# A hybrid decoder layer on one core: an ordered queue of loads and vector-engine weight sums in the down product, two buffers for early results, and stores moved to SyncE

## The chip, the cores and the metric

The kernel runs on one core of a Trainium2 chip. Its engines are TensorE (matrix products, PE in the rows; PEld is its weight load), VectorE (DVE), ScalarE (ACT), GpSimd (POOL) and SyncE (SP), each with its own queue of instructions, which it takes in order. "ACTq" and "SPq" in a row are transfers that ScalarE or SyncE issues. The metric is device time in microseconds (us), the median of several runs. The span of a profiled execution is the time from its first to its last instruction.

## The reference, cut to what matters

One decoder layer on x of shape (1, 1024, 1024): a token mixer, then a SwiGLU feed-forward, each with sandwich RMS norms and gates from a condition vector. The part around the change is the end of the mixer and the feed-forward.

```python
x = x + ga_m * rms_norm(concat(o_a, o_b) @ w_out, g_post_mix)
h = rms_norm(x, g_pre_ffn) * (1.0 + sc_f) + sh_f
gate, up = split(h @ w_gate_up)                 # 1024 x 2816 each
y = (silu(gate) * up) @ w_down                  # 2816 x 1024
x = x + ga_f * rms_norm(y, g_post_ffn)
```

## The kernel before, in words

Every float32 product is made of three products of split operands: `split` (lines 118 and 121) writes a rounded high half (a cast on ScalarE) and the rest as a low half (a subtraction on VectorE or GpSimd), and TensorE multiplies high by high, high by low and low by high. Tiles that hold such pairs are `wgu` (up weights), `hbo`, `hbs` (the activations h and their sums) and `hl` (down part).

The two feed-forward products are computed with seven block products instead of eight, named "1" to "7". Each needs sums of blocks of the weights and of the activations, and sums of the results.

**The end of the mixer.** `out_tile` makes the eight row tiles of x; `mod` and the loop over `k` that follows make h and the block sums T1 to T4 and B22 from it, on ScalarE and VectorE. For the first seven of the 22 column blocks f of the up product (`EARLY`), `early(f)` already multiplies blocks "1" and "2" while these sums are still being made: `product` with B11 into a PSUM bank, a copy of the bank into the left half of a tile `pr`, `product` with B21 onto the same bank, SiLU into the right half, and a store of the tile to `early_d` in DRAM by ScalarE's queue. For f below 3 `pr` is one of two `pair` tiles; for f from 3 to 6 it is the one tile `G_m`.

**The up part.** The loop over `order` takes the remaining block products of all f, 12 matmuls each: "67543" for the early f, "1627543" for the others, 140 in all. `prepare` keeps `LOOK` = 7 weight blocks ready ahead, in eight `wgu` tiles: four in the pool `fab0`, four in `fab1`, whose memory is that of the pool `outp` (`tm`, `G_m`, `xt2`, `HB`). `sources(f)` loads four `rawg` tiles by SyncE's queue and forms four sums on GpSimd (lines 1182 to 1185). VectorE adds up the results (lines 1302 to 1313), GpSimd multiplies (1310, 1315), and `act_sums` forms the activation blocks of the down product (1247, 1253, 1255, 1257), which `store` writes to `asd` in DRAM by ScalarE's queue, 77 blocks of 256 KB. Between them, `ada_acc(5, ...)` forms the gate of the last norm: 16 loads into the `rawg` ring and 16 multiply-adds on VectorE (lines 325, 327).

**The down part.** For w in "162754" and then "3", and for k from 0 to 10, `left` loads an activation block (`adr`, a ring of four) and splits it, `right` brings the weight block and splits it, and `down` issues 12 matmuls (line 1391). The `hl` tiles are a ring of ten, so five k at most are ready ahead. `WE[k]` (`we`) and `WD[k]` (`wo`) hold the weights of k. `right` loads a whole row block of 512 KB (line 1365) for "1", and 256 KB each for "6" and "2" (line 1368). Weight sums run on GpSimd (lines 1374, 1380) and on VectorE (1370, 1372, 1382). `finish` loads x again (`xt`), adds, and stores the output.

The order in each queue is fixed at build time by the framework's list scheduler, which places instructions by its own model of time and by priorities (`low` lowers one), so the code's order isn't the queue's order: a load may be placed well ahead of its use, and in front of loads that are needed sooner.

Of the kernel before, what the change touches and what calls it, by code (L numbers as in the profile page):

```python
# [13 lines left out]
P = 128  # L14
SEQ = 1024
NT = SEQ // P
D = 1024
# [30 lines left out]
def hybrid_layer(ctx, tc, x, c, w_ada, b_ada, g_pre_mix, g_post_mix, g_pre_ffn, g_post_ffn, w_in,  # L48
# [1037 lines left out]
    def pair():  # L1086
        return fsum.tile([P, 2, 512], F32, name="pair", bufs=2)
# [73 lines left out]
    def early(f):  # L1161
        ws = [weights(2 * f + h) for h in range(2)]
        bank = ps_O() if f % 2 else ps_S()

        pr = pair() if f < 3 else op_.tile([P, 2, 512], F32, name="G_m", bufs=1)
        product(bank, ws[0], B11, True, False)
        S.copy(pr[:, 0], bank)  # L1167
        product(bank, ws[1], B21, False, True)
        S.activation(pr[:, 1], bank, AF.Silu)
        nc.scalar.dma_start(early_d[f], pr)  # L1170
# [24 lines left out]
    for t in range(4, NT):  # L1195
        out_tile(t)
        if t > 4:
            early(t - 5)
    T2 = block(otp[1], "o")
    T3, T4 = (block(h2p, "s%d" % j) for j in (3, 4))  # L1200
    T1, B22 = (block(sl, "s%d" % j) for j in (1, 2))
# [35 lines left out]
    even = {}  # L1237

    def store(w, m, a):
        nc.scalar.dma_start(asd[AI[w], m], a)  # L1240

    def act_sums(f, a):

# [41 lines left out]
    for n, (f, w) in enumerate(order):  # L1285
        prepare(n + LOOK)
        early_act(n + 3)
        q = st_.setdefault(f, {})
        key = {"1": "X", "2": "X", "6": "Z", "7": "Z", "4": "Z", "5": "W", "3": "W"}[w]
        if w in "165":  # L1290
            q[key] = {"X": ps_S, "Z": ps_T, "W": ps_O}[key]()
        bank = q[key]
        product(bank, blks.pop(n), HBK[w], w in "165", w in "243")
        if w == "1":
            q["p1"] = half_t("p1", 3)
            S.copy(q["p1"], bank)
        elif w == "2":
            q["act"] = act_t()
            S.activation(q["act"][:, 0:512], bank, AF.Silu)
        elif w == "6":  # L1300
            q["u2"] = half_t("u2", 2)
            V.tensor_tensor(q["u2"], bank, q["p1"], op=OP.add)
        elif w == "7":
            q["u3"] = half_t("u3", 2)
            V.tensor_tensor(q["u3"], bank, q["p1"], op=OP.add)  # L1305
        elif w == "5":
            V.tensor_tensor(q["u3"], bank, q["u3"], op=OP.add)
        elif w == "4":
            V.tensor_tensor(q["p1"], bank, q["p1"], op=OP.add)
            G.tensor_tensor(q["act"][:, 0:512], q["act"][:, 0:512], q["p1"], op=OP.mult)  # L1310
            store("12"[f % 2], f // 2, q["act"][:, 0:512])
        else:
            V.tensor_tensor(q["u2"], bank, q["u2"], op=OP.add)
            S.activation(q["act"][:, 512:1024], q["u2"], AF.Silu)
            G.tensor_tensor(q["act"][:, 512:1024], q["act"][:, 512:1024], q["u3"], op=OP.mult)
            act_sums(f, q["act"])
            st_.pop(f)
        if w == "3" and f == 8:
            acc5 = fca.tile([P, SEQ], F32, name="acc5")
            with low(ADALOW):  # L1320
                ada_acc(5, acc5, fraw, "rawg", 512, 7, nc.sync)
        if w == "3" and f == 11:
            ada_sum(5, acc5)
    for name in ("fca", "fab1", "sl", "fab0", "fsum", "fraw"):
        L.pop(name)
# [20 lines left out]
    nc.gpsimd.dma_start(G_f.rearrange("p a b -> p (a b)"), bcast(gmd, D, D))  # L1346
    X, Z = [ps_S(), ps_S(), ps_T(), ps_T()], [ps_T(), ps_O(), ps_O(), ps_O()]

    def f32(tl, h):
        return tl[:, h, :]  # L1350

    def left(w, k, hl):
        ar = dr.tile([P, 512], F32, name="adr", bufs=4)
        nc.sync.dma_start(ar, asd[AI[w], k])
        split(hl[:, 0], hl[:, 1], ar, S, V)
        return hl

# [2 lines left out]

    def right(w, k):

        e, o = WE[k], WD[k]
        if w == "1":
            nc.sync.dma_start(e.rearrange("p a b -> p (a b)"), w_down[0, 2 * k * P:(2 * k + 1) * P, :])
        elif w in "62":
            h = int(w == "6")
            nc.sync.dma_start(f32(o, h), w_down[0, (2 * k + 1) * P:(2 * k + 2) * P, h * 512:(h + 1) * 512])
        if w == "6":
            V.tensor_tensor(e0(k), f32(o, 1), e0(k), op=OP.subtract)  # L1370
        elif w == "7":
            V.tensor_tensor(f32(e, 1), f32(o, 1), f32(e, 1), op=OP.subtract)
        elif w == "5":
            G.tensor_tensor(e0(k), f32(o, 1), e0(k), op=OP.subtract)
        src = {"1": e0(k), "6": e0(k), "2": f32(o, 0), "7": f32(e, 1), "5": e0(k), "4": f32(o, 0), "3": f32(o, 1)}[w]

        hl = ring() if w != "3" else dw.tile([P, 2, 512], F32R, name="wh", tag=f"we{k}")
        split(hl[:, 0], hl[:, 1], src, S, V)
        if w == "1":
            G.tensor_tensor(e0(k), f32(e, 1), e0(k), op=OP.subtract)  # L1380
        elif w == "2":
            V.tensor_tensor(f32(o, 0), f32(o, 0), e0(k), op=OP.subtract)
        return hl

    def e0(k):
        return f32(WE[k], 0)

    def down(bank, A, B, k, js, first, last):
        for j in js:
# [7 lines left out]
    def finish(t, ca, cb):  # L1397

        tk_ = slice(t * P, (t + 1) * P)
        xt = df.tile([P, D], F32, name="xt3", bufs=3)  # L1400
        nc.sync.dma_start(xt, x2d[tk_, :])
        G.tensor_scalar(ssd[:, t, 2:3], ssd[:, t, 0:1], 1.0 / D, 1e-6, op0=OP.mult, op1=OP.add)
        G.tensor_scalar(ssd[:, t, 3:4], ssd[:, t, 1:2], 1.0 / D, ssd[:, t, 2:3], op0=OP.mult, op1=OP.add)
        r = df.tile([P, 1], F32, name="rfr", bufs=3)
# [99 lines left out]
```

## Time and profile before

| | us |
|---|---|
| median of 3 runs (1574.71 to 1579.72) | 1575.67 |
| the profiled execution, its own time | 1578.7 |
| its span | 1576.7 |
| TensorE busy in it | 1453.8 (92%) |
| VectorE busy | 1203.6 (76%) |
| ScalarE busy | 875.1 (55%) |
| GpSimd busy | 740.3 (47%) |

The profiled execution is one of its own, 3.0 us above the median of the runs; its own time holds 2.0 us around the span. In the timeline, a row is an instruction or a run of like ones, and the bracket says how long its engine sat idle before it and what ended the wait.

### The profile page before, as it was taken

Reading aid. Unit: us, or ns where it says so; the run is one execution under the profiler, and the core shown is the slowest. Engines: PE = TensorE matmul, PEld = TensorE weight load, DVE = VectorE, ACT = ScalarE, POOL = GpSimd, SP = SyncE. Lnnn points to the kernel's source line nnn. Section 1 sums busy time; section 2 is a strip of 40 time slices with the busy share of each in tenths; the row PEclk is TensorE's granted clock in tenths of the full one; section 3 lists DMA queues with packets and bytes.
Section 4 is the critical chain, followed back from the end, with each engine's and each line's share of the span. In section 5 each row is a group of like instructions: output and inputs, shape, how many; then the busy total and the mean of one; then the engine's idle time right before and its main releaser. Section 6 shows DMA issues by size and latency. Waiting matters only on the chain.

```text
span 1576.7 us, 23672 instructions
## 1 busy us (share of the span) xinstructions
PE 1453.8 (92%) x7841; PEld 1232.7 (78%) x7841; DVE 1203.6 (76%) x2639; ACT 875.1 (55%) x1848; POOL 740.3 (47%) x1000
## 2 busy tenths in 40 slices
PE   3899998997889999899999879999999999799998
PEld 3789898996667877788887757887888888588886
DVE  6888988997999998778765585678556544878657
ACT  3447678966777877678774762222323322344543
POOL 2584353646877666355554325654444443423003
PEclk9999999996899999999999888999999999999999
DMA  9471351200000001211126554556333233943335
GB/s 305 147 233 28 60 156 38 85 2 9 9 13 1 1 13 48 67 35 41 41 97 236 192 163 133 161 159 187 102 97 113 92 99 109 372 139 97 98 110 191
DMA packets 141417, 168.65 MB, mean 107 GB/s; under 512 B 17440, under 2 KB 92544, under 8 KB 141168
## 3 DMA queue, kind: packets, MB, share of 16 engines
q1 hardware_dynamic: 119584, 127.60, 26.2%
q10 hardware_dynamic: 21072, 37.43, 6.5%
q0 software_dynamic: 640, 2.13, 0.4%
q8 instruction: 61, 1.00, 0.3%
q14 instruction: 60, 0.49, 0.1%
HBM read 126.71 MB, written 40.41 MB: 106 GB/s over the span
## 4 chain that ended last, share of the span: by engine, by line
PE 57%; DVE 22%; DMA 8%; ACT 6%; issue 4%; POOL 2%; ACTq 0%; SPq 0%; DVEq 0%; POOLq 0%
PE pT L1158 10%; PE pO L1158 7%; PE pS L1158 6%; PE pO L1391 4%; PE pT L1391 4%; PE pS L1391 3%; DVE tk_j L470 3%; DVE p L729 3%; DVE ptl L742 2%; DMA wt<-in_w_ada_dram 2%; PE pT L837 2%; PE pS L721 2%; PE pO L272 2%; PE pO L273 2%; PE pO L274 2%
## 5 line engine op out<-in xcount | busy, mean ns | idle before, releaser
L742 DVE TENSOR_TENSOR ptl<-pT,ptl 128x512 fp32r<-128x512 f32 x228 | 139.6, 625 | 31.7 <-ACT ptl L741 30.7
L1158 PE MATMUL pO<-hbs,wgu 128*128 128x512 f32 x564 | 139.6, 394 | 7.0 <-ACT G_m L1167 7.0
L741 ACT CAST ptl<-pT 128x512 fp32r<-128x512 f32 x228 | 117.6, 541 | 43.2 <-PE pO L842 18.7
L118 ACT CAST wgu<-pair 128x512 fp32r<-128x512 f32 x88 | 53.8, 620 | 153.8 <-PE pT L1158 69.8
L1158 PE MATMUL pT<-hbs,wgu 128*128 128x512 f32 x528 | 128.8, 393 | 4.6 <-DVE u L1305 4.6
L1158 PEld LDWEIGHTS pO<-hbs,wgu 128*128 128x128 f32 x564 | 107.6, 191 | 30.0 <-ACT G_m L1167 7.4
L272 PE MATMUL pO<-wsp,hT 128*128 128x256 f32 (+1 forms) x416 | 120.8, 292 | 10.2 <-ACT kvt L607 4.8
L273 PE MATMUL pO<-wsp,hT 128*128 128x256 f32 (+1 forms) x416 | 119.9, 289 | 5.1 <-DVE wsp L121 5.1
L1158 PEld LDWEIGHTS pT<-hbs,wgu 128*128 128x128 f32 x528 | 99.9, 190 | 26.6 <-DVE u L1305 5.9
L274 PE MATMUL pO<-wsp,hT 128*128 128x256 f32 (+1 forms) x416 | 119.1, 287 | 0.0
L825 POOL TENSOR_SCALAR p<-p,stat,gates 128x640 f32<-128x640 f32 (+7 forms) x128 | 106.3, 845 | 23.2 <-DVE stat L737 16.4
L732 ACT ACTIVATE p<-p,stat 128x640 f32<-128x640 f32 (+7 forms) x128 | 94.0, 736 | 26.7 <-DVE stat L731 17.2
L121 DVE TENSOR_TENSOR wgu<-pair,wgu 128x512 fp32r<-128x512 f32 x88 | 73.4, 839 | 38.1 <-ACT wgu L118 37.9
L118 ACT CAST hl<-adr 128x512 fp32r<-128x512 f32 x77 | 47.5, 623 | 96.4 <-PE pO L1391 40.5
L538 ACT ACTIVATE tk_j<-scores,tk_s 128x384 bf16<-128x384 f32 (+2 forms) x93 | 87.1, 937 | 10.0 <-DVE tk_s L480 3.7
L272 PEld LDWEIGHTS pO<-wsp,hT 128*128 128x128 f32 x416 | 81.1, 196 | 12.6 <-ACT kvt L607 5.6
L118 ACT CAST wgu<-rawg 128x512 fp32r<-128x512 f32 x66 | 40.6, 620 | 85.9 <-PE pT L1158 40.5
L273 PEld LDWEIGHTS pO<-wsp,hT 128*128 128x128 f32 x416 | 81.3, 196 | 6.7 <-DVE wsp L121 5.8
L470 DVE TENSOR_SCALAR_CACHE_REDUCE tk_j<-scores,tk_v 128x512 bf16<-128x512 f32 (+2 forms) x96 | 83.9, 874 | 0.6
L721 PE MATMUL pS<-KK,qst 128*128 128x512 f32 (+3 forms) x192 | 78.0, 411 | 6.8 <-DVE stat L729 6.5
L837 PE MATMUL pT<-ident,p 128*128 128x128 f32 x528 | 82.5, 279 | 1.8 <-POOL p L825 1.2
L1182 POOL TENSOR_TENSOR pair<-rawg 128x512 f32<-128x512 f32 x22 | 29.0, 1319 | 116.2 <-DVE wgu L121 110.2
(498 smaller groups left out, 4615.0 us busy)
## 6 DMA issues: line engine op xcount, KB each, us to landing
rawg<-in_w_gate_up_dram SPq DMA_DIRECT2D x102, 256.0 KB, 3.4
adr<-asd SPq DMA_DIRECT2D x77, 256.0 KB, 2.7
asd<-act ACTq DMA_DIRECT2D x66, 256.0 KB, 3.0
raw<-in_w_in_dram SPq DMA_DIRECT2D x36, 256.0 KB, 2.9
xt<-in_x_dram SPq DMA_DIRECT2D x16, 512.0 KB, 6.2
wt<-in_w_ada_dram SPq DMA_DIRECT2D x32, 256.0 KB, 4.5
wt<-in_w_ada_dram SPq DMA_DIRECT2D x16, 512.0 KB, 5.2
we<-in_w_down_dram SPq DMA_DIRECT2D x11, 512.0 KB, 6.2
```

Of the source, the lines that this page charges most:

```text
L118: S.copy(hi, src)
L272: PE.matmul(o, lh, rh, start=first, stop=False)
L273: PE.matmul(o, lh, rl, start=False, stop=False)
L274: PE.matmul(o, ll, rh, start=False, stop=last)
L470: V.tensor_scalar(tkj[0][:, :w], score(i0 + j), thr(j), 0.0, op0=op, op1=OP.add, accum_out=cnt[:, j:j + 1])
L721: PE.matmul(s[:, :c1 - c0], q, kh[:, c0:c1], start=True, stop=False)
L741: S.copy(hl[:n_rows, 0, :width], src[:n_rows, :width])
L742: V.tensor_tensor(hl[:n_rows, 1, :width], src[:n_rows, :width], hl[:n_rows, 0, :width].bitcast(F32), op=OP.subtract)
L825: G.tensor_scalar(self.p4[:, r, :n], self.p4[:, r, :n], stat[:, 2, r:r + 1], gates[:, i, c0 + r:c0 + r + 1], op0=OP.mult, op1=OP.mult)
L837: PE.transpose(pt[:, r * P:(r + 1) * P], self.p4[:, r, k * P:(k + 1) * P], ident)
L1158: PE.matmul(bank, blk[:, a, k, :], hb[:, k, b, :], start=first and k + a + b == 0, stop=k == KH_ - 1 and a == 1, skip_group_check=True)
L1391: PE.matmul(bank[j], A[:, a, j * P:(j + 1) * P], B[:, b, :], start=first and k + a + b == 0, stop=last and k == NP - 1 and a == 1, skip_gr ...
```

## The change

It does five things:

- early results of f = 3 to 6 alternate between two tiles, `G_m` and one slot of `xt2`;
- the 77 stores of the activation blocks are issued by SyncE instead of ScalarE;
- the gate's sums (`ada_acc(5)`) stand three f later in the code;
- all loads of the down part are put in a chain, each to be issued after the one before it in the code (`tc.issue_after` sets an order on the queue, it is no wait for the data); the weights are loaded as 256 KB quarters of the matrix where they are first needed: one for "1", two for "6", one for "2";
- the weight sums of the down part are formed in another order, all on VectorE (four per k: two in "6", one in "2", one in "5"); GpSimd has none.

```diff
-        pr = pair() if f < 3 else op_.tile([P, 2, 512], F32, name="G_m", bufs=1)
+        pr = pair() if f < 3 else prs[f % 2]
...
+    prs = [op_.tile([P, 2, 512], F32, name="G_m", bufs=1),
+           op_.tile([P, D], F32, name="xt2", bufs=5).rearrange("p (a b) -> p a b", a=2)]
...
     def store(w, m, a):
-        nc.scalar.dma_start(asd[AI[w], m], a)
+        nc.sync.dma_start(asd[AI[w], m], a)
...
-        if w == "3" and f == 8:
+        if w == "3" and f == 11:
             acc5 = fca.tile([P, SEQ], F32, name="acc5")
...
-        if w == "3" and f == 11:
+        if w == "3" and f == 14:
             ada_sum(5, acc5)
...
+    chain = [None]
+
+    def load(dst, src):
+
+        if chain[0] is None:
+            chain[0] = nc.sync.dma_start(dst, src)
+        else:
+            with tc.issue_after(chain[0].ins):
+                chain[0] = nc.sync.dma_start(dst, src)
...
-        nc.sync.dma_start(ar, asd[AI[w], k])
+        load(ar, asd[AI[w], k])
...
-        e, o = WE[k], WD[k]
+        b11, b12, b21, b22 = WE[k][:, 0], WE[k][:, 1], WD[k][:, 0], WD[k][:, 1]
         if w == "1":
-            nc.sync.dma_start(e.rearrange("p a b -> p (a b)"), w_down[0, 2 * k * P:(2 * k + 1) * P, :])
-        elif w in "62":
-            h = int(w == "6")
-            nc.sync.dma_start(f32(o, h), w_down[0, (2 * k + 1) * P:(2 * k + 2) * P, h * 512:(h + 1) * 512])
-        if w == "6":
-            V.tensor_tensor(e0(k), f32(o, 1), e0(k), op=OP.subtract)
-        elif w == "7":
-            V.tensor_tensor(f32(e, 1), f32(o, 1), f32(e, 1), op=OP.subtract)
+            load(b11, w_rows(k, 0, 0))
+        elif w == "6":
+            load(b12, w_rows(k, 0, 1))
+            load(b22, w_rows(k, 1, 1))
+            V.tensor_tensor(b12, b22, b12, op=OP.subtract)
+            V.tensor_tensor(b11, b12, b11, op=OP.add)
+        elif w == "2":
+            load(b21, w_rows(k, 1, 0))
         elif w == "5":
-            G.tensor_tensor(e0(k), f32(o, 1), e0(k), op=OP.subtract)
+            V.tensor_tensor(b11, b22, b11, op=OP.subtract)
...
-        if w == "1":
-            G.tensor_tensor(e0(k), f32(e, 1), e0(k), op=OP.subtract)
-        elif w == "2":
-            V.tensor_tensor(f32(o, 0), f32(o, 0), e0(k), op=OP.subtract)
+        if w == "2":
+            V.tensor_tensor(b21, b21, b11, op=OP.subtract)
...
-        nc.sync.dma_start(xt, x2d[tk_, :])
+        load(xt, x2d[tk_, :])
```

**ScalarE, the end of the mixer.** These are ten rows of ScalarE's queue before, the last two early results, f = 5 (bank `pO`) and f = 6 (bank `pS`); casts between them split the activation sums.

```order
L1167 COPY G_m_11244<-pO_11243 128x512
L118 CAST hbs4_11057<-HB_10465 128x512 x2
L118 CAST hbs3_11056<-tm_11272 128x512
L1169 ACTIVATE G_m_11244<-pO_11243 128x512
L118 CAST hbo_11055<-tm_11272 128x512
L1170 DMA earlyd_10426<-G_m_11244 128x1024
L118 CAST hbs4_11057<-HB_10465 128x512
L1167 COPY G_m_11310<-pS_11309 128x512
L1169 ACTIVATE G_m_11310<-pS_11309 128x512
L1170 DMA earlyd_10426<-G_m_11310 128x1024
```

And these are the rows for the same two results after the change.

```order
L1167 COPY G_m_11055<-pS_11308 128x512
L1169 ACTIVATE xt2_11056<-pO_11243 128x512
L118 CAST hbs2_11061<-tm_11271 128x512
L118 CAST hbs4_11059<-HB_10465 128x512
L1170 DMA earlyd_10426<-xt2_11056 128x1024
L118 CAST hbs1_11060<-HB_10465 128x512
L118 CAST hbo_11057<-tm_11206 128x512
L118 CAST hbs3_11058<-tm_11271 128x512
L1169 ACTIVATE G_m_11055<-pS_11308 128x512
L118 CAST hbs4_11059<-HB_10465 128x512
L1170 DMA earlyd_10426<-G_m_11055 128x1024
```

Before, the copy for f = 6 stands behind the store of f = 5 and writes the tile that it reads. Now the copy for f = 6 stands ahead of the SiLU and the store of f = 5, and writes another tile.

**SyncE, the first loads of the down part.** Before, while "1" runs, the queue reads like this from the fifth activation block on; `we` and `wo` are weights, and the 22 `wo` loads are all for "6" and "2".

```order
L1365 DMA we<-in_w_down_dram 128x1024
L1354 DMA adr<-asd 128x512
L1365 DMA we<-in_w_down_dram 128x1024
L1368 DMA wo<-in_w_down_dram 128x512
L1354 DMA adr<-asd 128x512
L1368 DMA wo<-in_w_down_dram 128x512
L1354 DMA adr<-asd 128x512
L1368 DMA wo<-in_w_down_dram 128x512 x15
L1354 DMA adr<-asd 128x512
L1368 DMA wo<-in_w_down_dram 128x512
L1354 DMA adr<-asd 128x512 x3
```

After the change the same place (k from 3 on in "1") reads as follows; the brackets name the semaphores that a row waits for, one of eight DMA semaphores in turn and those of engines, and the rows to `asd` are the last stores of the up part.

```order
L1243 DMA asd_11337<-act_14232 128x512 [waits DMAHW3_49,Pool_49]
L1360 DMA adr_14423<-asd_11337 128x512 [waits DMAHW4_49]
L1360 DMA we_14314<-in_w_down_dram 128x512 [waits DMAHW5_49]
L1360 DMA adr_14444<-asd_11337 128x512 [waits DMAHW6_49,DVE_49]
L1360 DMA we_14315<-in_w_down_dram 128x512 [waits DMAHW7_49,PE_49]
L1360 DMA adr_14465<-asd_11337 128x512 [waits DMAHW0_49,DVE_49]
L1360 DMA we_14316<-in_w_down_dram 128x512 [waits DMAHW1_49]
L1360 DMA adr_14486<-asd_11337 128x512 [waits DMAHW2_49,DVE_49]
L1243 DMA asd_11337<-act_14232 128x512 [waits DMAHW3_49,Pool_49]
L1360 DMA we_14317<-in_w_down_dram 128x512 [waits DMAHW4_49]
L1243 DMA asd_11337<-act_14115 128x512 [waits DMAHW5_49,DVE_49]
L1360 DMA adr_14507<-asd_11337 128x512 [waits DMAHW6_49,DVE_49]
```

The 15 weight loads in a row that stood ahead of an activation block are gone; activation and weight blocks alternate, and stores of the up part now stand among them. No row names the semaphore of the load just ahead of it.

**VectorE, the turn from "1" to "6" in the down part.** Before, the sums of "6" (lines 1370 and 1372) stand among the splits of "1" (k = 5 to 8 here).

```order
L121 TENSOR_TENSOR hl_14471<-adr_14472,hl_14471 128x512
L121 TENSOR_TENSOR hl_14477<-we_14318,hl_14477 128x512
L1370 TENSOR_TENSOR we_14313<-wo_14324,we_14313 128x512
L1372 TENSOR_TENSOR we_14313<-wo_14324,we_14313 128x512
L121 TENSOR_TENSOR hl_14493<-adr_14494,hl_14493 128x512
L121 TENSOR_TENSOR hl_14499<-we_14319,hl_14499 128x512
L1370 TENSOR_TENSOR we_14314<-wo_14325,we_14314 128x512
L1372 TENSOR_TENSOR we_14314<-wo_14325,we_14314 128x512
L121 TENSOR_TENSOR hl_14515<-adr_14516,hl_14515 128x512
L121 TENSOR_TENSOR hl_14521<-we_14320,hl_14521 128x512
```

After the change the sums (lines 1383 and 1384) begin only behind the last splits of "1" (k = 10, `we_14321`), and the split of "6" follows them.

```order
L121 TENSOR_TENSOR hl_14554<-we_14320,hl_14554 128x512
L121 TENSOR_TENSOR hl_14569<-adr_14570,hl_14569 128x512
L121 TENSOR_TENSOR hl_14575<-we_14321,hl_14575 128x512
L1383 TENSOR_TENSOR we_14311<-wo_14322,we_14311 128x512
L121 TENSOR_TENSOR hl_14594<-adr_14595,hl_14594 128x512
L1384 TENSOR_TENSOR we_14311<-we_14311 128x512
L121 TENSOR_TENSOR hl_14603<-we_14311,hl_14603 128x512
L121 TENSOR_TENSOR hl_14618<-adr_14619,hl_14618 128x512
L1383 TENSOR_TENSOR we_14312<-wo_14323,we_14312 128x512
L1384 TENSOR_TENSOR we_14312<-we_14312 128x512
```

## Rows read from the trace of the kernel before

**Rows 1.** The page: busy time of each engine, its share of the span, instructions.

```profile
PE 1453.8 (92%) x7841; PEld 1232.7 (78%) x7841; DVE 1203.6 (76%) x2639; ACT 875.1 (55%) x1848; POOL 740.3 (47%) x1000
```

**Rows 2.** Windows by stage: stretch, length, busy by engine, clock, DMA share, GB/s.

```profile
926.40:945.20 18.80, 8.77 (x33) 6.57 (x31) 18.70 (x31) 12.43 (x23) 0.00 (x0) 0.81 0.40 138
945.20:953.27 8.07, 5.49 (x13) 3.80 (x13) 0.02 (x1) 1.80 (x3) 0.00 (x0) 0.60 0.32 109
...
1346.10:1388.10 42.00, 32.57 (x125) 24.49 (x126) 39.61 (x46) 13.28 (x25) 21.42 (x13) 0.92 0.93 336
1388.10:1569.60 181.50, 181.44 (x801) 149.97 (x799) 134.18 (x195) 87.53 (x168) 28.91 (x33) 1.00 0.39 120
```

**Rows 3.** Timeline, TensorE, into the up part: start, length, instruction, [idle before, releaser].

```profile
937.16 4.97 PE L1158 MATMUL pO<-hbs,wgu 128*128 128x512 f32 x12 [6.97 <-ACT G_m L1167]
946.08 5.49 PE L1158 MATMUL pS<-hbs,wgu 128*128 128x512 f32 x12 [3.94 <-ACT G_m L1167]
953.27 4.49 PE L1158 MATMUL pT<-hbo,wgu 128*128 128x512 f32 x12 [1.70 <-ACT wgu L118]
957.56 3.32 PE L1158 MATMUL pO<-hbs,wgu 128*128 128x512 f32 x12
961.61 0.73 PE L1158 MATMUL pT<-hbo,wgu 128*128 128x512 f32 x2 [0.73 <-ACT wgu L118]
```

**Rows 4.** Timeline, VectorE and ScalarE in the same stretch.

```profile
942.80 0.33 ACTq L1170 DMA_DIRECT2D earlyd<-G_m  x1
...
944.48 0.69 DVE L121 TENSOR_TENSOR hbs<-HB,hbs 128x512 fp32r<-128x512 f32 x1
...
945.44 0.59 ACT L1167 COPY G_m<-pS 128x512 f32<-128x512 f32 x1 [0.99 <-DMA earlyd<-G_m]
...
952.60 0.62 ACT L118 CAST wgu<-pair 128x512 fp32r<-128x512 f32 x1 [0.40 <-ACT G_m L1169]
```

**Rows 5.** Timeline around the gate sum in the up part, ScalarE and TensorE.

```profile
1084.30 0.62 ACT L118 CAST wgu<-rawg 128x512 fp32r<-128x512 f32 x1 [8.65 <-POOL act L1310]
...
1091.81 4.49 PE L1158 MATMUL pT<-hbs,wgu 128*128 128x512 f32 x12 [3.27 <-DVE u L1305]
```

**Rows 6.** Waits of SyncE's queue, 960 to 1345 us: total, times, longest.

```profile
SPq L1178 <- DVE wgu L121: 127.1, 33, 11.1
```

**Rows 7.** Timeline, TensorE, the down part.

```profile
1343.20 2.88 PE L1158 MATMUL pO<-hbs,wgu 128*128 128x512 f32 x12
1347.16 0.73 PE L1391 MATMUL pS<-hl 128*128 128x512 f32 x2 [1.07 <-ACT hl L118]
...
1380.19 2.08 PE L1391 MATMUL pS<-hl 128*128 128x512 f32 x4 [4.75 <-DVE hl L121]
...
1553.06 8.32 PE L1391 MATMUL pS<-wh,hl 128*128 128x512 f32 x36
1561.22 8.32 PE L1391 MATMUL pT<-wh,hl 128*128 128x512 f32 x36
```

**Rows 8.** Timeline, the down part's first block of products, other engines.

```profile
1350.24 1.78 DVE L121 TENSOR_TENSOR hl<-adr,hl 128x512 fp32r<-128x512 f32 x1
...
1359.35 0.62 ACT L118 CAST hl<-adr 128x512 fp32r<-128x512 f32 x1 [8.60 <-DMA asd<-act]
...
1373.04 0.62 ACT L118 CAST hl<-adr 128x512 fp32r<-128x512 f32 x1 [9.43 <-DMA adr<-asd]
...
1378.85 0.68 DVE L121 TENSOR_TENSOR hl<-adr,hl 128x512 fp32r<-128x512 f32 x1
1379.46 0.68 DVE L121 TENSOR_TENSOR hl<-we,hl 128x512 fp32r<-128x512 f32 x1
```

**Rows 9.** Timeline, SyncE's queue, loads of the down part.

```profile
1355.13 12.16 SPq L1368 DMA_DIRECT2D wo<-in_w_down_dram  x15
...
1367.68 0.33 SPq L1354 DMA_DIRECT2D adr<-asd  x1
```

**Rows 10.** The page: DMA issues, KB each, us to landing.

```profile
adr<-asd SPq DMA_DIRECT2D x77, 256.0 KB, 2.7
```

More of the change, by code (lines that the diff above doesn't have):

```diff
@@ L1347, in hybrid_layer, with w_rows @@
     X, Z = [ps_S(), ps_S(), ps_T(), ps_T()], [ps_T(), ps_O(), ps_O(), ps_O()]
-    def f32(tl, h):
-        return tl[:, h, :]
+    chain = [None]
[5 more added lines that the diff above has]
+                chain[0] = nc.sync.dma_start(dst, src)
+    def w_rows(k, o, h):
+        r = (2 * k + o) * P
+        return w_down[0, r:r + P, h * 512:(h + 1) * 512]
     def left(w, k, hl):
         ar = dr.tile([P, 512], F32, name="adr", bufs=4)
-        nc.sync.dma_start(ar, asd[AI[w], k])
+        load(ar, asd[AI[w], k])
         split(hl[:, 0], hl[:, 1], ar, S, V)
@@ L1361, in right @@
     def right(w, k):
-        e, o = WE[k], WD[k]
+        b11, b12, b21, b22 = WE[k][:, 0], WE[k][:, 1], WD[k][:, 0], WD[k][:, 1]
         if w == "1":
-            nc.sync.dma_start(e.rearrange("p a b -> p (a b)"), w_down[0, 2 * k * P:(2 * k + 1) * P, :])
-        elif w in "62":
-            h = int(w == "6")
-            nc.sync.dma_start(f32(o, h), w_down[0, (2 * k + 1) * P:(2 * k + 2) * P, h * 512:(h + 1) * 512])
-        if w == "6":
-            V.tensor_tensor(e0(k), f32(o, 1), e0(k), op=OP.subtract)
-        elif w == "7":
-            V.tensor_tensor(f32(e, 1), f32(o, 1), f32(e, 1), op=OP.subtract)
+            load(b11, w_rows(k, 0, 0))
[6 more added lines that the diff above has]
+            load(b21, w_rows(k, 1, 0))
         elif w == "5":
-            G.tensor_tensor(e0(k), f32(o, 1), e0(k), op=OP.subtract)
-        src = {"1": e0(k), "6": e0(k), "2": f32(o, 0), "7": f32(e, 1), "5": e0(k), "4": f32(o, 0), "3": f32(o, 1)}[w]
+            V.tensor_tensor(b11, b22, b11, op=OP.subtract)
+        src = {"1": b11, "6": b11, "2": b21, "7": b12, "5": b11, "4": b21, "3": b22}[w]
         hl = ring() if w != "3" else dw.tile([P, 2, 512], F32R, name="wh", tag=f"we{k}")
         split(hl[:, 0], hl[:, 1], src, S, V)
-        if w == "1":
-            G.tensor_tensor(e0(k), f32(e, 1), e0(k), op=OP.subtract)
-        elif w == "2":
-            V.tensor_tensor(f32(o, 0), f32(o, 0), e0(k), op=OP.subtract)
-        return hl
-    def e0(k):
-        return f32(WE[k], 0)
+        if w == "2":
+            V.tensor_tensor(b21, b21, b11, op=OP.subtract)
+        return hl
     def down(bank, A, B, k, js, first, last):
```

## The prediction, made before the changed kernel ran

> **What bounds the kernel now.** The page comes first: TensorE is busy for 92% of the span [rows 1], so the whole change can win only what lies in the other 8%, and only where TensorE itself waits. Its own timeline from the end of the mixer on shows three such places. Twelve matmuls of a full-clock product take 2.72 us from start to start; the 36 between the last two rows of group 7 take 8.16, so one matmul is 0.2267 us [rows 7]. Against that measure each stretch is read.
>
> First, the way into the up part. TensorE idles 6.97 and 3.94 us for the copy into `G_m`, and 1.70 us for a cast [rows 3]; the granted clock of 945 to 953 us is 0.60, between its two levels of 1.2 and 2.4 GHz [rows 2]. The copy that starts at 945.44 waited for the store of `G_m` issued at 942.80 [rows 4]: an early result may be copied only when the one before it has left the only tile. The first product of the up part starts at 953.27 [rows 3].
>
> Second, the gate sum in the up part: 3.27 us of idle time at 1091.81, then twelve matmuls at a lower clock, 4.49 us long in the row [rows 5].
>
> Third, the start of the down part. From 1347.16 to 1561.22 there are 888 of its 924 matmuls [rows 7], worth 888 x 0.2267 = 201.3 us, in 214.1: 12.8 us are lost. The windows say where: 32.57 busy of 42.00 us up to 1388, and 181.44 of 181.50 from there on [rows 2]. In those 42 us the transfers are at 0.93 of their engines and 336 GB/s [rows 2]. The largest single hole is 4.75 us at 1380.19 [rows 7].
>
> **Part 1, two tiles for early results.** Before, f = 6 could be copied at 945.44 and its second product ran from 946.08; the cast that opens the up part stood behind its SiLU and came at 952.60 [rows 4]. With two tiles, the copy for f = 6 needs the store of f = 4, which is issued a whole result earlier; I place that second product near 934 to 937 (the ScalarE rows around it wait for VectorE's sums, not for a store). What is late next? The first product of the up part, "6", needs T2 of all four k. These come from VectorE, which was busy 18.70 of 18.80 us and finished its last split at 944.48 + 0.69 = 945.2 [rows 2, 4]. The change adds nothing to VectorE there, so that end stays, the opening cast can follow ScalarE's last one, behind which that split started at 944.48 [rows 4], and the first product starts at 945.0 instead of 953.27: 8.3 us earlier. The idle stretch ahead of it, some 7 us, leaves a low clock as before: the two products that open the up part took 953.27 to 960.88 for 24 matmuls, 7.6 us where 5.4 would do [rows 3]; I charge 0.3 us more than that. The 0.73 us at 961.61 [rows 3] should go, since the queue now has product "7" of f = 0 in front of that one: 8.3 - 0.3 + 0.7 = **8.7**. Bounds: 5 if the first weight block waits for the store of f = 6 (2.6 us from 942.80 to the copy at 945.44), 9.5 if the clock recovers sooner.
>
> **Part 2, stores on SyncE and the gate sum later.** ScalarE's queue no longer stops behind a store: 8.65 us before the cast at 1084.30 [rows 5] and 8.60 us at 1359.35 [rows 8]. Except for those two places this covered nothing, because TensorE had blocks ready. On SyncE the stores stand ahead of `rawg` loads. Those already waited 127.1 us for VectorE to free their slots [rows 6], and in the new queue a store of f stands ahead of loads for f + 3 or f + 4, with a product of f lasting 7 x 2.72 = 19 us; a store that is some us late has two f of cover. I take 0; without the cover the price would be the store's wait, up to 9 us once. The gate sum keeps its 16 loads and 16 VectorE instructions, now at f = 10 and 11. In the old place its stall cost 3.27 idle and 1.6 of clock (the row of twelve matmuls is 4.49 us long, that of a product at full clock 2.88 [rows 5, 7]): 4.9 in all. Half of its cause, ScalarE's stop, is gone; the other half, VectorE's load, stays, and now the sums of `act_sums` stand at its start, not its end. I take 2.5 of 4.9 won; bounds 4.9 won and 3 lost.
>
> **Part 3, the chain and the sums in the down part.** What held TensorE in those 42 us? Fifteen `wo` loads for "6" were issued in 12.16 us from 1355.13, with the next activation block of "1" behind them, at 1367.68 [rows 9]; ScalarE's cast waited 9.43 us for such a block until 1373.04 [rows 8]. In the same time VectorE ran sums of "6" before the splits that "1" needed, and its instructions took 1.78 us beside GpSimd's where 0.68 is usual [rows 8]. All three causes are taken away: loads come in order of use, sums behind the splits, and GpSimd's 22 subtractions are gone. Does the new order carry it? Loads: 15 blocks of 256 KB in 12.16 us are 0.81 us each. "1" needs two for each k, 1.6 us; "6" needs three, 2.4 us; "2" needs two; TensorE takes 12 x 0.2267 = 2.72 us for a k. VectorE: its rows start 0.61 us apart [rows 8]; "6" and "2" have four instructions for each k (the one of "5" runs ahead in "2"), 2.4 us against 2.72. Eleven instructions more in all, 6.7 us, hidden under 200 us of products; were they bare, that is their price. The four stores of the last f stand among loads of k = 3 to 8 of "1", and each waits for a sum that VectorE and GpSimd finish some 5 to 9 us after the first product begins, while TensorE needs k = 3 only 8 us after it and k = 8 after 22. So I leave 1.5 us of the 12.8 for the beginning: **11.3 won**. Bounds: 12.8, and 5 if "6" runs short of loads or of VectorE (2.4 against 2.72 is a thin margin: a tenth too slow costs nothing, a quarter, 3.0 against 2.72, costs 0.3 x 11 = 3 us for each of "6" and "2").
>
> At the border of the two parts TensorE idled 1.07 us for a cast [rows 7] that stood behind a store; the first block's cast may now come early. I take 0.5.
>
> **Sum.** 8.7 + 2.5 + 11.3 + 0.5 = 23.0 us off the profiled execution's own 1578.7. That execution lies 3.0 above the median of the runs, 1575.67, so the forecast is 1575.67 - 23.0 = 1552.7, say **1553**. The tail behind the last matmul is the same chain as before and keeps its time.
>
> **The rivals.** (a) *The down part stays transfer-bound.* For it: 0.93 of the transfer engines in that window [rows 2], "6" now moves 768 KB for each k where it moved 512, and the load for "1" comes in pieces half as large. Against: the window carried the loads of "6" and "2" as well, while "1" itself now asks for 512 KB in 2.72 us, 193 GB/s of the 336 seen, and "6" for 289. If half of the lost time stays, or a stall of the gate sum repeats in full: 1575.67 - 23 + 6 to 12 = 1559 to 1565. The Trainium skill speaks for this rival: "DMA: Bandwidth & Descriptors", section "Measured (HBM→SBUF, 128 partitions, SWDGE, issued from GpSimd)", asks for transfers of at least 1 MiB, since small ones are mostly fixed cost; its fixed 2.0 us (section "Anatomy of one DMA") would make the eleven extra loads 22 us if each were paid on the path, an estimate from that page that would leave nothing of the gain. The trace disagrees with such a sum here: at 256 KB one load lands in 2.7 us [rows 10], but 15 of them left the queue in 12.16 us.
>
> (b) *The change doesn't do what it says:* the second tile waits for something as late as the first, and the new loads queue behind memory that the up part frees late. Then parts 1 and 3 give a few us only: 1571 to 1580. Against: the slot of `xt2` was last read by the transposes of the first half of the rows, before all early results.
>
> (c) *The chain makes the loads serial, and the kernel slower.* If each load waited for the one ahead to land, 2.7 us [rows 10], "1" and "2" would take 5.4 us for a k and "6" 8.1 against 2.72: (2.7 + 2.7 + 5.4) x 11 = 118 us more, 1670 us. It turns into a loss once a load holds the queue for 1.46 us (77 loads in "1", "6" and "2", 112 us, against 33 x 2.72 plus the 23 won). Against: the new rows of SyncE's queue name, besides the buffer, only one of eight semaphores in turn, and 0.81 us was seen.
>
> **How the numbers follow.** The forecast has 0.70, with 1548 to 1558 its own range; (a) 0.22, (b) 0.05, (c) 0.03. The range to 0.8: the bounds of the terms reach to 9.5 + 4.9 + 12.8 + 1.1, some 28 won, 1547, to the upper half of (a), 1564. A difference of 0.3%, 4.7 us, is about what a measurement tells from none. Faster: all of the forecast and (a), a little of (b): 0.93; the same 0.04; slower 0.03.
>
> **What would show it.** The first product of the up part near 945, on a low clock for some 5 us; no ScalarE row that waits on a store to `asd`; at the gate sum a stall of 3 us or less; from the first product of the down part a window of 42 us with over 40 busy and less than 0.8 of the transfer engines. Wrong would be: TensorE waiting in "6" for VectorE or a load, the first product after 948, or a `rawg` load behind a store that GpSimd waits for.

## The result, and the profile after

The changed kernel takes 1551.5 us (median of 4 runs, 1550.34 to 1554.76), the one before 1576.4 in the same comparison: a ratio of 0.9843, with a 95% interval of 0.982 to 0.9866. The forecast was 1553. The profiled spans differ by 28.3 us (1576.7 and 1548.4), since the profiled execution of before lay above its median and that of after below.

The page, busy time by engine, answers to [rows 1]:

```profile
PE 1439.0 (93%) x7841; PEld 1222.6 (79%) x7841; DVE 1183.7 (76%) x2650; ACT 877.8 (57%) x1848; POOL 703.9 (45%) x978
```

Where the time came from is read by windows, from a row of twelve transposes that both kernels run at the same place of TensorE's queue (L185), to the first up product, to the first down product, to the last row of 36 matmuls. First the kernel before (columns as in [rows 2]):

```profile
921.77:953.27 31.50, 18.61 (x70) 13.81 (x68) 23.35 (x39) 18.86 (x34) 0.40 (x1) 0.78 0.46 147
953.27:1347.16 393.89, 387.49 (x1697) 318.90 (x1697) 243.54 (x309) 110.85 (x192) 185.18 (x127) 0.99 0.41 131
1347.16:1561.22 214.06, 205.69 (x888) 167.89 (x889) 166.98 (x230) 98.30 (x187) 48.70 (x42) 0.98 0.48 157
```

and the kernel after:

```profile
919.27:942.39 23.12, 13.62 (x69) 10.89 (x68) 23.04 (x39) 18.62 (x35) 0.00 (x0) 0.90 0.65 199
942.39:1330.21 387.82, 386.09 (x1696) 318.88 (x1697) 237.71 (x308) 113.08 (x193) 187.04 (x127) 0.99 0.39 124
1330.21:1532.87 202.66, 201.58 (x889) 166.59 (x888) 153.47 (x242) 99.35 (x185) 12.15 (x20) 1.00 0.57 185
```

The three stretches are 8.38, 6.07 and 11.40 us shorter. The remaining 2.5 us (921.77 against 919.27) lie ahead of every row that the change moves, and say nothing of it. One thing has to be put right between the last two: before, TensorE idled ahead of its first down matmul ([rows 7]: 3.96 us from 1343.20 to 1347.16, where 2.72 would do), now behind the fourth. With that 1.24 counted to the down part in both, the gains are 8.4, 4.8 and 12.6, 25.8 in all; by the medians the change is worth 24.9.

TensorE's timeline after the change answers to [rows 3, 5, 7]:

```profile
931.57 3.02 PE L1158 MATMUL pS<-hbs,wgu 128*128 128x512 f32 x12 [1.70 <-ACT G_m L1167]
942.39 5.49 PE L1158 MATMUL pT<-hbo,wgu 128*128 128x512 f32 x12 [7.80 <-ACT wgu L118]
947.67 3.17 PE L1158 MATMUL pO<-hbs,wgu 128*128 128x512 f32 x12
950.68 2.88 PE L1158 MATMUL pT<-hbs,wgu 128*128 128x512 f32 x12
...
1129.50 3.01 PE L1158 MATMUL pT<-hbs,wgu 128*128 128x512 f32 x12 [1.17 <-DVE u L1305]
...
1330.21 0.61 PE L1400 MATMUL pS<-hl 128*128 128x512 f32 x2
1330.66 0.61 PE L1400 MATMUL pT<-hl 128*128 128x512 f32 x2
1332.36 1.20 PE L1400 MATMUL pS<-hl 128*128 128x512 f32 x4 [1.08 <-DVE hl L121]
...
1532.87 8.32 PE L1400 MATMUL pT<-wh,hl 128*128 128x512 f32 x36
```

The two waits for the copy into `G_m` (6.97 and 3.94) have become one of 1.70. The wait behind them has grown to 7.80, and the first up product still comes 8.4 us sooner. Behind 1332.36 there is no idle row left in the down part.

What ends last ahead of the first up product is read from the chain of work of that stretch, its last pieces (start, us, what):

```profile
939.36 1.20 DVE hbs L121 x2
940.56 0.61 DVE HB L1215
941.18 0.02 issue
941.20 0.62 ACT hbs L118
941.82 0.53 ACT wgu L118
942.35 0.04 issue
942.39 2.93 PE pT L1158 x6
```

From 924.91 on, that chain is VectorE's alone (22 of its 28 pieces), then one cast of sums and the opening cast of a weight block, as the prediction had it. The two opening products took 8.29 us (942.39 to 950.68) for 24 matmuls that want 5.44; the granted clock of that stretch is the row below. The second row is the first 42 us of the down part, against [rows 2]:

```profile
942.39:950.68 8.29, 8.29 (x24) 6.44 (x25) 6.41 (x8) 3.69 (x7) 5.83 (x4) 0.65 0.59 180
1330.21:1372.21 42.00, 40.92 (x181) 33.56 (x180) 35.99 (x56) 22.01 (x38) 2.20 (x2) 1.00 0.95 332
```

TensorE has 40.92 us of work there where it had 32.57, and the transfer engines are as full as before: 0.95, 332 GB/s. Not all that was lost before was waiting: of the 214.06 us of the old down part TensorE was busy for 205.69, with matmuls that want 201.3, so 8.4 us were idle and 4.4 went to matmuls at a lower clock, granted 0.92 in those 42 us [rows 2]. Now the clock there is 1.00, 1.1 us are idle, and 201.58 us are busy.

The waits of SyncE's queue in the up part after the change (line waited for, us in total, times, longest) answer to [rows 6]:

```profile
SPq L1243 <- POOL act L1313: 112.6, 20, 14.3
SPq L1178 <- DVE wgu L121: 83.4, 30, 8.6
```

The stores (line 1243) wait for GpSimd's products on this queue now, with loads behind them, and the loads of line 1178 wait less for VectorE than they did. None of ScalarE's waits, in the up part or the first 42 us of the down part, is for a store to `asd` any more; before, it stopped for 8.65 us with a store ahead that waited for GpSimd, and for 8.60 us for a store at the start of the down part [rows 5, 8].

### The profile page after: what moved, and what is told of

Same layout as the page of the kernel before. It is cut to its first block, busy times and chain, and to the rows that moved or that the text cites. A ratio compares the mean times of both kernels' runs of the same rounds, so it can differ in the third digit from the quotient of the medians.

```text
span 1548.4 us, 23692 instructions
## 1 busy us (share of the span) xinstructions
PE 1439.0 (93%) x7841; PEld 1222.6 (79%) x7841; DVE 1183.7 (76%) x2650; ACT 877.8 (57%) x1848; POOL 703.9 (45%) x978
## 4 chain that ended last, share of the span: by engine, by line
PE 59%; DVE 22%; DMA 6%; ACT 6%; issue 5%; POOL 3%; ACTq 0%; DVEq 0%; SPq 0%; POOLq 0%
PE pT L1158 11%; PE pO L1158 8%; PE pS L1158 6%; PE pT L1400 4%; PE pO L1400 4%; PE pS L1400 3%; DVE tk_j L470 3%; DVE p L729 3%; DVE ptl L742 2%; PE pT L837 2%; PE pO L272 2%; PE pS L721 2%; PE pO L274 2%; PE pO L273 2%; DMA wt<-in_w_ada_dram 2%
```

## The experiments

Besides the medians, each is read by the lengths of the three stretches in its own trace: "entry" (twelve transposes to first up product: 31.50 before, 23.12 after), "up" (393.89, 387.82) and "down" (first down product to last row: 214.06, 202.66; its 888 matmuls alone want 201.3). What exceeds 201.3 is called lost; where the wait of 1.1 us at the border lies behind the first down matmul, 1.4 of the loss are that. These lengths repeat better than the medians: five executions with the down part of the kernel after (it and the last four runs below) gave 202.66 to 202.69, three with that of before 213.25 to 214.97, and the entry with one tile 30.76 to 31.50. Where two runs are compared whose ratios have overlapping intervals, the difference is shown by the traces alone.

**The parts one by one, on the kernel before.** The edits are the hunks of the change shown ahead: `prs`; `store` on SyncE; f = 11 and 14; `load`, `w_rows`, `right`.

> The kernel before with the second tile for early results alone. Theory: the part pays by itself, because the way into the up part ends with VectorE's last split of T2 and no longer with the store of G_m: the first up product starts 8 to 9 us sooner, counted from the last transposes of the mixer, and the median falls by 8.4 +- 1 us (1568 us). Rival: the gain needs the stores off ScalarE's queue or the later gate sum (the 8 us come back as a wait in the first products of the up part): under 4 us.

Measured: 1567.7 against 1576.8, ratio 0.9941 (0.9923 to 0.9958). Entry 23.26, up 394.20, down 214.97. The theory holds: 8.2 us of the entry, and no new wait comes up behind it; the up part is 0.3 and the down part 0.9 us longer in this execution, with TensorE's waits in the down part as before.

> The kernel before with the 77 stores on SyncE alone. Theory: worth nothing by itself where TensorE has blocks ready; what it can win is the half of the gate sum's stall that came from ScalarE's stop behind a store, so 0 to 3 us (1573 to 1576), with the stall at the gate sum down from 5.0 (idle and low clock) to 2 to 3 us. Rival: ScalarE's stops cost the down part too (8.60 us ahead of a cast there), and the loads of the down part behind the stores come later or sooner: a change of more than 4 us either way, seen in the first 42 us of the down part.

Measured: 1573.5, ratio 0.9977 (0.9965 to 0.999). The gate sum's stall is 2.25 us idle and a row of 4.61 instead of 3.27 and 4.49; 12.2 us are lost in the down part (1.4 at the border), 1.8 less than before with the border counted. 3.3 us by the median (the interval reaches from 1.6 to 5.5), where the theory gave 0 to 3. One stall of TensorE in the down part is gone with the stores, 1.72 us at 1360.54 in the trace of before, behind the cast that had stopped for 8.60 us [rows 8]. TensorE's waits there go from 9.4 to 8.6 us only, border included, since the one for the next late block grew from 1.45 to 3.07. The rest of the 1.8 is matmuls at a lower clock: 3.6 us lost to them here, 4.4 before, and 5.3 and 3.5 in the runs with the tile and the gate alone, whose down part is that of before.

> The kernel before with the gate sum at f = 11 and 14 alone. Theory: half of the stall is ScalarE's stop, the other half VectorE's load; moving the sums by itself takes 0 to 2.5 us off (1574 to 1576), and a stall of 2 to 5 us stands at the new place. Rival: the place alone is the cause and the stall goes to 1.5 us, as in the kernel after: 3.5 us off and ScalarE's stop without a price.

Measured: 1575.2, ratio 0.9992 (0.9979 to 1.0005): no difference clear of noise. At the new place TensorE waits 2.20 us and a row takes 4.60. TensorE's row at the gate sum with the stores moved alone, and with the place moved alone:

```profile
1087.77 4.61 PE L1158 MATMUL pT<-hbs,wgu 128*128 128x512 f32 x12 [2.25 <-DVE u L1305]
1141.04 4.60 PE L1158 MATMUL pT<-hbs,wgu 128*128 128x512 f32 x12 [2.20 <-DVE u L1302]
```

The place alone isn't the cause: alone it leaves 4 us of stall, the stores alone leave 4, both together leave 1.3.

> The kernel before with the down part alone (chain, quarter loads, sums on VectorE). Theory: order of loads and sums inside the down part is the whole cause there: the 12.8 us lost behind the first down product go to under 2, median 12 +- 1 us lower (1564). Rival: the stores of the up part on ScalarE's queue hold the first casts (8.60 us before), and without their move 3 us or more of the loss stay: 1567 or above.

Measured: 1565.8, ratio 0.9929 (0.9909 to 0.9948). Down 201.46: 0.2 us lost. The down part's loss is removed by its own edits, wherever the stores are. The four gains by the medians, 9.2 + 3.3 + 1.6 + 11.1, add up to 25.2, the change to 24.9. That isn't because the parts don't touch each other: the stores and the place win 0.9 and 1.0 us of the gate sum's stall alone and 3.6 together, while what the stores alone win in the down part is lost time that the down edits remove too. The two nearly cancel, and the 1.6 is within its noise.

**Chain or sums?** The chain taken out of the kernel after:

```diff
-        if chain[0] is None:
-            chain[0] = nc.sync.dma_start(dst, src)
-        else:
-            with tc.issue_after(chain[0].ins):
-                chain[0] = nc.sync.dma_start(dst, src)
+        nc.sync.dma_start(dst, src)
```

> The kernel after without the chain: its loads may be placed as the list scheduler likes; quarter loads and VectorE sums stay. Theory: the order of the loads is the first cause, so a good part of the 12.8 us comes back: 6 to 12 us lost behind the first down product, 1558 to 1563. Rival: the sums (GpSimd's subtractions beside VectorE, and sums ahead of splits) were the cause: no more than 2 us come back, under 1554.

Measured: 1557.2, ratio 0.9874 (0.9858 to 0.989). Down 208.96: 7.7 lost, 1.4 of it at the border, so 6.3 for the chain. Its trace in "6", SyncE's queue, ScalarE and TensorE:

```profile
1364.13 4.39 SPq L1354 DMA_DIRECT2D wo<-in_w_down_dram  x7
...
1371.06 1.00 SPq L1354 DMA_DIRECT2D xt<-x2d  x2
...
1372.46 5.68 SPq L1354 DMA_DIRECT2D adr<-asd  x4
...
1376.45 0.62 ACT L118 CAST hl<-adr 128x512 fp32r<-128x512 f32 x1 [6.35 <-DMA adr<-asd]
...
1377.65 0.50 PE L1394 MATMUL pT<-hl 128*128 128x512 f32 x1 [3.47 <-ACT hl L118]
```

Weights for "2" and even the x of the kernel's very end (`xt`) stand ahead of an activation block of "6", the same picture as in [rows 9]. In this run VectorE's sums of "6" stand among its splits of "1" again (the first at 1344.85, with eight splits of "1" still to come).

The sums and load sizes of before, kept in the chain (in the kernel after, `right` as it was, with `load` for the transfers):

```diff
+            load(e.rearrange("p a b -> p (a b)"), w_down[0, 2 * k * P:(2 * k + 1) * P, :])
...
+            G.tensor_tensor(e0(k), f32(e, 1), e0(k), op=OP.subtract)
```

> The kernel after with the weight sums and load sizes of before (512 KB for 1, 256 KB for 6 and 2, 22 subtractions on GpSimd), all loads in the chain. Theory: with the loads in order most of the gain holds; GpSimd's subtractions fall in 1 and 5, each beside VectorE's splits: 1 to 4 us lost, 1552 to 1556. Rival: 512 KB rows for 1 and slow VectorE rows beside GpSimd are what held TensorE: 5 us or more lost in the first 42 us, 1557 or above.

Measured: 1553.5, ratio 0.9848 (0.9833 to 0.9863). Down 204.33: 3.0 lost, 1.4 of it at the border. The groups of its first 42 us (count, busy, mean ns) show why: the splits of weight blocks take 1267 ns each on VectorE, beside eleven subtractions of GpSimd, where the kernel after has 687 for the same instruction (second fence).

```profile
L121 DVE TENSOR_TENSOR hl<-we,hl 128x512 fp32r<-128x512 f32 x15 | 19.0, 1267 | 0.1
L1393 POOL TENSOR_TENSOR we<-we 128x512 f32<-128x512 f32 x11 | 18.4, 1676 | 9.5 <-DVE hl L121 8.8 <-PE pT L1404 0.7
```

```profile
L121 DVE TENSOR_TENSOR hl<-we,hl 128x512 fp32r<-128x512 f32 x18 | 12.4, 687 | 1.3 <-ACT hl L118 1.1
```

The chain alone on the kernel before, everything else old:

> The kernel before with all loads of the down part in the chain and nothing else: 512 KB rows for 1, the weight sums of before with 22 subtractions on GpSimd, stores on ScalarE. Theory from the two runs that took one of chain and sums back: the chain does most of it, since it also puts the sums of 6 behind the splits of 1 on VectorE; the 12.8 us lost behind the first down product go to 2 to 4, median 9 to 11 us lower. Rival: chain and sums only work together (each taken back alone lost 6.3 and 1.7 us, 8.0 of 12.6), so the chain alone leaves 6 us or more.

Measured: 1567.5, ratio 0.9931 (0.9913 to 0.9949). Down 203.81 (1347.32 to 1551.13): 2.5 lost of 12.8. By losses without the border: neither 12.8, chain alone 2.5, new sums and quarter loads without it (stores moved) 6.3, both 0 to 0.2. The rival falls: the chain does four fifths by itself. The shares taken back alone (6.3 and 1.7) were no measure of it, since either edit mends a part of the same loss.

What the chain orders isn't the loads alone, though. VectorE before, where the largest hole of the down part is (first and last of ten sums of "6" in a row), and, below, its first sum of "6" in the run with the chain alone:

```profile
1372.83 0.68 DVE L1370 TENSOR_TENSOR we<-wo,we 128x512 f32<-128x512 f32 x1
...
1378.25 0.68 DVE L1372 TENSOR_TENSOR we<-wo,we 128x512 f32<-128x512 f32 x1
```

```profile
1374.71 1.77 DVE L1380 TENSOR_TENSOR we<-wo,we 128x512 f32<-128x512 f32 x1
```

Before, the cast of the late activation block ended at 1373.04 + 0.62 = 1373.66, but its split came only at 1378.85, behind those ten sums, and TensorE waited 4.75 us for that split [rows 7, 8]. With the chain alone all 22 splits of "1" stand ahead of the first sum. So the largest hole was VectorE's order more than a late load; how the chain's gain divides between the order of the loads and that of the sums, no run here shows.

**Are the transfers the limit?** Loads that nothing needs, on the kernel after (the quarter is loaded again for "2"):

```diff
             load(b11, w_rows(k, 0, 0))
+            load(b21, w_rows(k, 1, 0))
...
             load(b22, w_rows(k, 1, 1))
+            load(b21, w_rows(k, 1, 0))
```

> The kernel after with a third load of 256 KB for each k of 1 and a fourth for each k of 6 (the lower left quarter, which 2 loads again), 5.8 MB more. It asks whether the transfers, at 0.95 of their engines in the first 42 us, bound the down part. Theory: they don't; the share is high since loads run ahead of their use. 1 would then ask for 289 GB/s and 6 for 386 where stretches of 10 us showed 383 to 388, so with the lead of some k TensorE waits under 3 us, 1551 to 1555. Rival: the transfers are at their limit already and each extra load is paid, 22 x 0.7 = 15 us: 1560 or above.

Measured: 1555.3, ratio 0.9853 (0.9834 to 0.9872). Down 207.08: 5.8 lost, 4.4 more than in the kernel after. Neither figure: the 5.8 MB are 15 us of transfer at the rate of the row below, and two thirds of that is hidden. By the ratios this run can't be told from the kernel after; the 4.4 is read from the traces. The stretch in which TensorE waits, and ScalarE's waits in the first 43 us:

```profile
1339.00:1371.29 32.29, 29.71 (x126) 22.97 (x125) 18.08 (x28) 14.61 (x25) 0.00 (x0) 1.00 1.05 391
```

```profile
ACT hl L118 <- DMA adr<-asd: 16.2, 7, 6.6
```

At 391 GB/s and 1.05 of the transfer engines TensorE does wait for casts that wait for loads. The kernel after has two windows at nearly that rate, and the same wait of ScalarE in its first 42 us:

```profile
1340.00:1350.00 10.00, 10.00 (x46) 8.29 (x45) 5.84 (x10) 6.06 (x10) 0.00 (x0) 1.00 1.04 388
1350.00:1360.00 10.00, 10.00 (x46) 8.29 (x45) 8.42 (x15) 4.16 (x8) 0.00 (x0) 1.00 1.04 383
```

```profile
ACT hl L118 <- DMA adr<-asd: 6.3, 3, 4.9
```

TensorE is busy throughout these windows: ScalarE waits 6.3 us for loads, but blocks are ready ahead. Neither the share nor the rate shows that the transfers are the limit; TensorE's own waits do.

**What bounds the entry, and a faster version.** Four splits moved to GpSimd, which is idle there:

```diff
-        split(B22[:, k, 0, :], B22[:, k, 1, :], b22, S, V)
+        split(B22[:, k, 0, :], B22[:, k, 1, :], b22, S, G)
```

> The kernel after with four of the splits ahead of the up part (low half of B22) on GpSimd, which sits idle there for 24.9 us. Theory: VectorE's rows set the first up product, and they get 4 x 0.61 = 2.4 us fewer; but a VectorE row beside one of GpSimd's took 1.78 us where 0.68 is usual, so four such meetings give 4.4 back: the first up product between 1 us sooner and 3 us later. Rival: VectorE and GpSimd don't disturb each other there, and the 2.4 us are won in full (1549); or VectorE isn't what ends last, and nothing moves (under 0.3 us).

Measured: 1554.9, ratio 0.9856 (0.9828 to 0.9883); entry 25.62, 2.5 us longer than after. In the range of the theory, but not only by slow VectorE rows. GpSimd's last such split, and VectorE's row that waited for it:

```profile
940.78 0.68 DVE L1211 TENSOR_TENSOR HB<-tm,HB 128x512 f32<-128x512 f32 x1
940.79 6.01 POOL L121 TENSOR_TENSOR hbs<-tm,hbs 128x512 fp32r<-128x512 f32 x1 [3.49 <-ACT hbs L118]
...
945.00 0.68 DVE L121 TENSOR_TENSOR hbs<-HB,hbs 128x512 fp32r<-128x512 f32 x1
...
946.83 0.69 DVE L1214 TENSOR_TENSOR tm<-tm,HB 128x512 f32<-128x512 f32 x1 [1.15 <-POOL hbs L121]
```

VectorE's rows run on at 0.68 us, and GpSimd's one instruction ends 1.12 us after VectorE's last of them (945.00 + 0.68).

Eight early results instead of seven, to use the 7.8 us in which TensorE waits:

```diff
-    EARLY = 7
+    EARLY = 8
...
-        early(k + 3)
+        for f in ((3, 4), (5,), (6,), (7,))[k]:
+            early(f)
```

> The kernel after with eight early results instead of seven (two of them with the first k of the sums). It uses the 7.8 us for which TensorE waits ahead of the up part. 24 matmuls, 5.4 us, move out of the up part; VectorE, which sets the end of that wait, gets two weight splits more, 1.2 us, and the two products run partly at a low clock. Theory (VectorE's last split of T2 sets the first up product): first up product 1 to 2 us later, up part 5.4 us shorter: 3 to 4.5 us faster, 1547 to 1548.5. Rival: ScalarE's extra casts and copies come behind that chain and delay it by 3 us or more: gain under 2 us, 1549.5 or above.

Measured: 1552.6, ratio 0.9839 (0.9825 to 0.9853): no gain. Counted from the row of twelve matmuls 40.62 us ahead of the first up product in the kernel after (901.77), that product comes at 43.16, 2.5 us later; the up part is 385.27, only 2.6 us shorter. Not ScalarE's casts took the rest: the gate sum stalls TensorE for 3.96 us with a row of 5.30 behind it. So that sum was spread:

```diff
-                ada_acc(5, acc5, fraw, "rawg", 512, 7, nc.sync)
-        if w == "3" and f == 14:
+                ada_acc(5, acc5, fraw, "rawg", 512, 7, nc.sync, (0,))
+        if w == "3" and f == 15:
+            with low(ADALOW):
+                ada_acc(5, acc5, fraw, "rawg", 512, 7, nc.sync, (512,))
+        if w == "3" and f == 18:
```

> The kernel after with the gate's sixteen multiply-adds in two halves, eight at f = 11 and eight at f = 15, the sum at f = 18. Theory: the stall that is left at the gate sum (1.17 us idle and 0.13 of clock) is VectorE's load: its multiply-adds stand between the evictions that TensorE waits for. Eight in a row of products are no longer late: the stall goes to under 0.3 us, the up part is 1 to 1.5 us shorter, median 1550 to 1551. Rival: each half stalls TensorE once, or the loads into the rawg ring hold up weights: the up part stays at 387.8 us or grows.

Measured: 1551.0, ratio 0.9841 (0.9817 to 0.9866): by the median no difference from the kernel after. In the trace no idle row is left in TensorE's queue at either place, and the up part is 386.66, 1.2 us shorter; the entry of this execution is 0.3 us longer, so the step is shown in the trace alone.

> Eight early results and the gate's sums in two halves. Theory: with eight early results the up part had 24 matmuls fewer, but the gate sum stalled TensorE for 3.96 us and the clock fell for 2.6 more; that stall is a matter of which f the multiply-adds fall on, not of the early result. With halves it goes: first up product 2.5 us later than in the kernel after, up part 5.4 + 1.3 us shorter, 4.2 us faster: 1547 to 1548. Rival: the eighth result leaves VectorE or ScalarE behind for the whole early range, and the stall comes back elsewhere: 1550 or above.

Measured: 1545.2 (4 runs, 1541.97 to 1548.37), ratio 0.9795 (0.9771 to 0.982), the fastest of all; up 380.08, 7.7 us shorter than after, first up product 2.5 us later. The theory holds, and the median lies below its 1547 to 1548: the traces' 7.7 less 2.5 make 5.2 us, the medians 6.3. One stall of 0.83 us for VectorE, at 1190.29, is left in the middle of the up part.

## Why the prediction was right, by its own steps

- **Part 1, 8.7 us.** Entry 8.4 in the trace (8.3 predicted), 8.2 with that edit alone. On the old trace's time axis, 2.50 us later, the first product comes at 942.39 + 2.50 = 944.9; 945.0 was predicted, from VectorE's last split. The low clock stayed: the first two products took 8.29 us where 7.6 were seen before [rows 3] and 7.9 were charged, and with the 0.73 stall that did go the opening is worth 0.1 to 0.2, not 0.4. How dear that clock is varies: with nearly the same wait ahead, the two products took 7.1 us in the runs with the tile alone and with the extra loads, 8.2 to 8.3 in others. The second product of f = 6 came at 931.57 + 2.50 = 934.1, in the 934 to 937 given.
- **Part 2, 2.5 us.** The mechanism was right, both halves of the cause exist (each edit alone leaves a stall of 4 us), but the term was too small: the sum's stall went from 4.9 to 1.3, 3.6 won, and behind its opening the up part gained 4.7 in all, with the small waits for VectorE that the sum didn't count. The mistake was to halve the stall: with both causes gone it doesn't halve, since either alone is enough to make TensorE late. That the stores cost nothing on SyncE held: they wait 112.6 us for GpSimd, and TensorE waits for none of it. But GpSimd waits once, 3.2 us at 1016.98, for a `rawg` load that left the queue behind three stores: a sign that the prediction had named for being wrong came up, and cost TensorE nothing.
- **Part 3, 11.3 us and 0.5 at the border.** 12.6 together. The margins that the working called thin held: no wait of TensorE in "6". The working gave three causes for the loss; the trace puts most of the largest hole down to the second, sums of "6" ahead of the splits (1373.66 to 1378.85, shown above), and 4.4 us of the 12.8 were no wait but matmuls at a lower clock, which the working didn't tell apart. The border term was wrong in its place: a stall of 1.1 us is still there, now for a split on VectorE instead of a cast on ScalarE, and the 1.5 that were left for the beginning are this one.
- **"Less than 0.8 of the transfer engines"** was wrong: 0.95. The step took a full transfer window for a sign of the transfer-bound rival; it is the sign of loads that run ahead. What tells the two apart is whether TensorE waits for an engine that waits on a load, as in the run with extra loads at 391 GB/s.
- **The rivals.** (a) did not occur: the down part lost nothing to loads, though 5.8 MB more bring it about. The rule of the Trainium skill that spoke for it ("DMA: Bandwidth & Descriptors", section "Measured (HBM→SBUF, 128 partitions, SWDGE, issued from GpSimd)") asks for 1 MiB a transfer, by loads that GpSimd issued; here transfers of 256 KB from SyncE's queue reached 391 GB/s over 32 us, so the trace does not bear it out for this queue. (b) and (c) are out by the result.

In all, 25.8 us in the traces stand against the 23.0 of the sum: some 2 of the difference is part 2, nearly 1 part 3 with the border. That the forecast of 1553 lies within 2 us of 1551.5 is no luck of errors that cancel; all but part 1 were too small.

Shown by runs: the tile, the down edits and the chain each gave their share alone. Not shown: how much of the chain's share is the order of the loads and how much that of VectorE's sums; and the 1.8 us of the stores alone in the down part, of which 0.9 are waits and the rest is within what the clock varies.

## What to carry to other kernels

Where a list scheduler fills a queue, look for loads of a later stage ahead of a block that is needed now; a chain that only fixes the order of issue recovered four fifths of the loss here, at no cost in instructions, and it put the sums that hang on those loads in order too. So look in the queues of the computing engines as well for work of a later stage ahead of what is needed now. Transfer engines at 0.95 are a bound only if the engine on the path waits, in the end, for a load, so look at its waits first. Two causes of one stall can each be enough for most of it: the gain of removing both is then more than the gains of each.

## What was not expected of the hardware

An instruction of GpSimd that met a row of VectorE instructions without a gap took 6.01 us, where the first of its kind in the same run took 1.48: it ended only after VectorE had run out of work (the run with B22 on GpSimd). GpSimd's spans are rough, but VectorE's own wait of 1.15 us for the result bears it out. In the run with the old sums it was VectorE's rows that grew, to 1267 ns in the mean. So either engine can be the one that yields.

The Trainium skill, "SBUF — State Buffer", section "Who interferes with whom", says that a VectorE instruction with two inputs in SBUF contends with a GpSimd instruction that reads SBUF, and section "SBUF: two separate sides" that the one that starts first holds the shared ports for its whole instruction. The traces agree with the first. By the second alone GpSimd would wait for one VectorE instruction, 0.6 us; here it waited for eight.
